# Moving the split weights of an encoder block by 64 bytes against their partner operand

## The chip, the cores and the metric

The kernel runs on one core of one Trainium2 chip. The metric is the device time of one execution in microseconds (us). Before the change it is 1420.87 us, the median of 3 runs (1420.75 to 1421.65).

## The reference

One layer of a streaming encoder over 512 tokens of width 2048, all in float32. Cut to what matters:

```python
h = rmsnorm(x, norm_w)                                   # (512, 2048)
a_q, a_f, a_i, a_g, c_q, c_kv, k_idx, w_idx, b_g, m_a, m_b = split(h @ w_in)   # w_in: 2048 x 10128
y_a = rmsnorm(hgrn2_recurrence(silu(a_q), 1 - f(a_f), log f(a_f), a_i)) * silu(a_g)  # 8 heads of 128
q, q_idx = (rmsnorm(c_q) @ w_uq), (rmsnorm(c_q) @ w_qidx)     # c_q has 512 columns
k, v = split(rmsnorm(c_kv) @ w_ukv)
y_b = attention(q, top_k(indexer(q_idx, k_idx, w_idx)) of (k, v), rel_bias) * silu(b_g)
merged = sigmoid(m_a) * (y_a @ w_pa) + sigmoid(m_b) * (y_b @ w_pb)
out = rmsnorm(x + merged @ w_out) * final_norm_w
```

Nearly all of the arithmetic is products of 512 tokens with weight matrices.

## The kernel before

**Split products.** TensorE multiplies float32 numbers in a fast format with a shorter mantissa (`float32r`, FR in the code). To keep float32 accuracy each operand is split into a high part and the rest: `split` (L66) writes the high part with ScalarE (ACT, L67) and the rest with VectorE (DVE, L68). A product is then three matmuls, written by `mm3` (L70): high by high (L71), one rest by high (L72), high by the other rest (L73). In each matmul one operand, 128 columns wide, is loaded into the array by a weight load (LDWEIGHTS, the engine row PEld): the **stationary** operand. The other streams through it, 256 or 512 columns here: the **moving** operand. In the profile a matmul is named out<-moving,stationary, or the other way round; which is which is in the code: the first operand of `PE.matmul(ps, l, r)` is the stationary one. Each matmul has its own weight load, which runs while the matmul ahead of it streams.

**Where the work lies.** Weights come in pieces of at most 128 x 1024 float32 by DMA (SyncE's queue, SP) into tiles `wr` of the pool `weights`, and are split into the tiles `wh` and `wl` of that pool. `specs` lists the pieces in the order of use. `prep(i)` (L149) splits pieces up to two ahead of the one in use; the pool has three buffers of `wh` and `wl`. TensorE's order is the program's order. Small work of other stages (attention, the recurrence, top-k) is pumped in between by `pump`.

The program's stages that matter here:

- **Gate units** (`pair_job`, `pair_unit`, L929 and after): 11 units of 8 steps; each step has 42 matmuls of 256 columns (7 products of Strassen's scheme, 2 column halves, 3 matmuls). Seven products need three plain blocks of the weights (split into `bh`, `bl`) and four sums of blocks (`pair_sums`: VectorE L138 to L140 adds, then `wh`, `wl`). Weights are stationary, the tokens (`xh`, `xl`, and their sums `sh`, `sl`) move. At the end of a unit `gate_pair_evac` (L970) takes the seven sums out of PSUM: VectorE L975 to L981. For the first four units, whose gate is a silu, VectorE also multiplies four times (L987) by a sigmoid of ScalarE, in the unit after. Seven of the eight PSUM banks are in use, so a unit's fifth product needs a bank that L979 of the evacuation sets free.
- **a_i jobs** (`ai_job`): 3 jobs of 192 matmuls of 256 columns. The tokens are stationary, the weights `wh`, `wl` move.
- **Out units** (`out_job`, `pair_unit` with `tokens_out`): 3 units of 8 steps of 42 matmuls of 256 columns for 1536 of the 2048 output columns. The merged tokens (`mh`, `ml`, and their sums `so`) are stationary, the weights (`bh`, `bl`, `wh`, `wl`) move.
- **Other products** have 512 columns (`feat_job`: weights stationary, tokens move) or 384 (the indexer's). Of those, `uqkv` multiplies the normalised c_q (`cqh`, `cql`) by w_uq: 96 matmuls of 512 columns in 4 jobs.

Of the kernel before, what the change touches and what calls it, by code (L numbers as in the profile page):

```python
# [26 lines left out]
F32 = mybir.dt.float32  # L27
FR = mybir.dt.float32r
# [6 lines left out]
T, D = 512, 2048  # L35
# [3 lines left out]
NEG = -1e30  # L39
GONE = -3e38  # L40
WCAP = 1024
MO = (0, 128, 384, 768)


@with_exitstack
def hybrid_block(ctx, tc, x, norm_w, w_in, lb_table, gnorm_a, q_norm_w, kv_norm_w, w_uq,
# [3 lines left out]
    V, A, G, PE, SP = nc.vector, nc.scalar, nc.gpsimd, nc.tensor, nc.sync  # L50
# [25 lines left out]
        PE.matmul(ps, l, r, start=first, stop=last, skip_group_check=True)  # L76


    ident = const.tile([128, 128], F32, name="ident")
    levels = const.tile([128, 6, 32], U8, name="levels")  # L80
    A.dma_start(ident, c_ident)
    ones = const.tile([128, 128], F32, name="ones")
    G.memset(ones, 1.0)
    ones_r = const.tile([128, 128], FR, name="ones_r")
    G.tensor_copy(ones_r, ones)
    eps = const.tile([128, 1], F32, name="eps")
    G.memset(eps, EPS)
    cols = const.tile([128, 32], F32, name="cols")
# [16 lines left out]
    def enter(name, side=None, space=None):  # L105
        cm = tc.tile_pool(name=name, bufs=1, side=side, reuse_waits="tile")
        pools[name] = (cm, cm.__enter__())
        return pools[name][1]
# [4 lines left out]
    R = SimpleNamespace()  # L113
# [14 lines left out]
    def load_ahead():  # L128
        while issued[0] < min(issued[1] + 2, len(specs)):
            load(issued[0])  # L130
            issued[0] += 1

    def pair_sums(t):


        b = t.rearrange("p (q n) -> p q n", q=4)
        sv = R.g.tile([128, 4, 256], F32, name="sv", bufs=R.sv)
        V.tensor_tensor(sv[:, 0:2, :], b[:, 1:3, :], b[:, 0:1, :].to_broadcast([128, 2, 256]), op=OP.add)  # L138
        V.tensor_tensor(sv[:, 2, :], sv[:, 1, :], b[:, 1, :], op=OP.add)  # L139
        V.tensor_tensor(sv[:, 3, :], sv[:, 2, :], b[:, 3, :], op=OP.add)  # L140
        bh = R.g.tile([128, 3, 256], FR, name="bh", bufs=3)
        bl = R.g.tile([128, 3, 256], FR, name="bl", bufs=3)
        split(bh, bl, b[:, 1:4, :])
        vh = wpool.tile([128, 4, 256], FR, name="wh")
        vl = wpool.tile([128, 4, 256], FR, name="wl")
        split(vh, vl, sv)
        return bh, bl, vh, vl

    def prep(i):  # L149
        while issued[1] < min(i + 3, len(specs)):  # L150
            j = issued[1]
            if specs[j][3:] == ("pair",) and not hasattr(R, "g"):
                open_pairs()
            load_ahead()
            _, kc, n = specs[j][:3]
            t = raws.pop(j)
            if specs[j][3:] == ("pair",):
                halves[j] = pair_sums(t)
                issued[1] += 1
                continue  # L160
            if len(specs[j]) > 3:
                both = R.s2.tile([128, 2, WCAP], FR, name="wk", tag=specs[j][3])
                hi, lo = both[:, 0, :], both[:, 1, :]
            else:
                hi = wpool.tile([128, WCAP], FR, name="wh")
                lo = wpool.tile([128, WCAP], FR, name="wl")
            split(hi[:, :kc * n], lo[:, :kc * n], t[:, :kc * n])
            halves[j] = tuple(a[:, :kc * n].rearrange("p (k n) -> p k n", k=kc) for a in (hi, lo))
            issued[1] += 1
# [26 lines left out]

    jobs, hg = [], {}

    def feat_job(src, col, ntile, nk, kc, rhs, evac, before=None, width=T, after=None):
        at = len(specs)  # L200
        n = ntile * 128
        for k in range(0, nk, kc):
            specs.append(([(0, n, src[k * 128:(k + kc) * 128, col:col + n])], kc, n))

        def run():
            if before:
                before()
            ps = [mmp.tile([128, T], F32, name="acc")[:, 0:width] for _ in range(ntile)]
            for i in range(nk // kc):
                prep(at + i)  # L210
                wh, wl = halves.pop(at + i)
                for c in range(ntile):
                    for k in range(kc):
                        kk = i * kc + k
                        rh, rl = rhs(kk)
                        s = slice(c * 128, c * 128 + 128)
                        mm3(ps[c], wh[:, k, s], wl[:, k, s], rh, rl, kk == 0, kk == nk - 1)
                    if kk == nk - 1:
                        evac(c, ps[c])
                    if ntile < 4 or c % 2:  # L220
                        pump()
                if after and i in after:
                    after[i]()

        jobs.append(run)
# [8 lines left out]
    def start():  # L234
        R.v0 = enter("v0")
        p0 = enter("p0", side="right")
        HF = D // 2
        nw = p0.tile([16, 128], F32, name="nw")
        wc = p0.tile([128, 16], F32, name="wc")
# [3 lines left out]
        sq = p0.tile([128, HF], mybir.dt.bfloat16, name="sq")  # L243
        st = p0.tile([128, 4, 4], F32, name="st")
        rows = p0.tile([128, 128], F32, name="rows")
        wh = [p0.tile([128, 4, 272], FR, name=f"fh{i}") for i in range(4)]
        wl = [p0.tile([128, 4, 272], FR, name=f"fl{i}") for i in range(4)]
        raw = [None] * 4
# [167 lines left out]
    def open_branches():  # L416
        R.v = enter("values")
        R.s = enter("shared")
        R.q = enter("idx", side="right")
        R.M = R.s.tile([128, 1280], F32, name="M")  # L420
        R.ckh = R.s.tile([128, 2, T], FR, name="ckh")
        R.ckl = R.s.tile([128, 2, T], FR, name="ckl")
        lev = R.q.tile([128, 6, 32], F32, name="lev", tag="bf")
        SP.dma_start(lev, c_levels.rearrange("p (l t) -> p l t", l=6))
        G.tensor_copy(levels, lev)
# [159 lines left out]
    def ai_job(p):  # L585
        at = len(specs)
        c0 = 2048 + p * 256
        for k in range(0, NK, 4):
            specs.append(([(0, 256, w_in[k * 128:(k + 4) * 128, c0:c0 + 256])], 4, 256))

        def run():
            ps = [mmp.tile([128, T], F32, name="acc") for _ in range(2)]
            for i in range(4):
                prep(at + i)
                wh, wl = halves.pop(at + i)
                for k in range(4):
                    kk = i * 4 + k
                    rh, rl = x_rhs(kk)
                    for t in range(4):
                        s = slice(t * 128, t * 128 + 128)  # L600
                        mm3(ps[t // 2][:, (t % 2) * 256:(t % 2) * 256 + 256], rh[:, s], rl[:, s],
                            wh[:, k, :], wl[:, k, :], kk == 0 and t % 2 == 0, kk == NK - 1)
                    if k % 2 == 1:
                        pump()
            v = hg[p, "v"] = R.v.tile([128, 4, 256], F32, name="hv", bufs=2)
            for i in range(2):
                A.activation(v[:, 2 * i:2 * i + 2, :], ps[i].rearrange("p (t n) -> p t n", t=2), AF.Copy)

        jobs.append(run)
# [24 lines left out]
    def hgrn_gen(p):  # L634
# [54 lines left out]
        for c in range(2):  # L689
            pt = bank("hkt")  # L690
            for j in range(3):
                PE.transpose(pt[:, j * 128:(j + 1) * 128], k[:, c, j * 128:(j + 1) * 128], ident)
            A.activation(kd[:, c], pt[:, :384].rearrange("p (j t) -> p j t", j=3), AF.Copy)
        yield
        st = R.h.tile([128, 2, 3, 128], F32, name="hst")
# [138 lines left out]
    def att_turn(blocks):  # L834
        bk = [bank("tA"), bank("tB"), bank("tC")]
        hi = R.a.tile([128, 1280], FR, name="PT")
        for kt in range(4):
            for b in range(kt, 4):
                o = PT_AT[kt] + (b - kt) * 128
                PE.transpose(bk[o // 512][:, o % 512:o % 512 + 128],  # L840
                             blocks[b][:, kt * 128:kt * 128 + 128], ident)
        lo = R.a.tile([128, 1280], FR, name="P")
        for i, o in enumerate((0, 512, 1024)):
            s = slice(o, min(o + 512, 1280))
            split(hi[:, s], lo[:, s], bk[i][:, 0:s.stop - o])
        return hi, lo
# [56 lines left out]
    def open_pairs():  # L903
        drain("norm")
        drain("misc")
        leave("norms")
        R.g = enter("pairs")
        R.sv = 2

    xs_h, xs_l = [], []  # L910

# [145 lines left out]
        feat_job(w_in, p * 256, 2, NK, 4, x_rhs, aq_evac(p))  # L1057

    def uqkv(p):
        feat_job(w_uq, p * 256, 2, 4, 4, c_rhs, uq_evac(p),  # L1060
                 before=None if p else (lambda: drain("top")))
        ukv_job(p)

# [59 lines left out]
    def open_merge():  # L1123
        drain("att")
        flush()
        flush()
        leave("att")
        leave("shared")
        leave("values")
        leave("us")  # L1130
        leave("ranks")
        R.m = enter("merged")
        R.s2 = enter("sums2")
        R.u = enter("us")
        R.g = enter("pairs", side="right")
        R.sv = 1
        load_gates(32, 0)
        load_gates(16, 0)

# [258 lines left out]
```

## Time and profile before

| | |
|---|---|
| median of 3 runs | 1420.87 us (1420.75 to 1421.65) |
| the profiled execution's own time | 1417.68 us |
| its span in the profile | 1415.9 us |
| busy share of the span | PE 98%, PEld 90%, DVE 75%, ACT 43%, POOL 6% |
| chain that ended last | PE 79%, DVE 11%, ACT 5%, DMA 2% |

Between span and own time lie 1.8 us. The profiled execution is 3.2 us below the median of the runs. Matmuls are pipelined, and the durations of the profile overlap: how fast TensorE gets on is read from the starts of successive matmuls.

### The profile page before, as it was taken

To read this page: it belongs to the slowest core of one execution; us is meant where nothing else is said; L and a number is where in the kernel's file an instruction comes from. 1 tells how busy PE (TensorE), PEld (TensorE's weight loads), DVE (VectorE), ACT (ScalarE), POOL (GpSimd) and SP (SyncE) were. 2 spreads that over 40 slices of the span, in tenths; PEclk is the share of its full clock that TensorE was granted. 3 is DMA by queue.
4 is the path that set the end of the run, shared out by engine and by line. 5 is a ranking of instruction groups with operands and counts; after the bars stand their busy time and mean duration, and the time that the engine had idled before them with its cause. 6 is when DMAs were issued, how large, how long until landed. Compare 5 with 4: busy or idle time off the path is not lost.

```text
span 1415.9 us, 25873 instructions
## 1 busy us (share of the span) xinstructions
PE 1392.4 (98%) x10652; PEld 1276.0 (90%) x10652; DVE 1059.4 (75%) x1736; ACT 606.9 (43%) x857; POOL 88.3 (6%) x85
## 2 busy tenths in 40 slices
PE   8999999999999999999999999999999999999997
PEld 7878999999999999997888889988888888899996
DVE  7877888889888887677769966577655438899856
ACT  6455444444444344564142352454353224443334
POOL 2100000000000000000201211213111000000000
PEclk9999999999999999999999999999999999999999
DMA  6223344444443444324324243334466556743554
GB/s 214 82 83 118 106 135 134 128 127 150 135 133 104 137 135 133 123 82 135 106 68 137 78 131 106 97 119 128 164 227 230 175 194 220 227 134 116 169 183 173
DMA packets 138776, 197.30 MB, mean 139 GB/s; under 512 B 9841, under 2 KB 82082, under 8 KB 138530
## 3 DMA queue, kind: packets, MB, share of 16 engines
q1 hardware_dynamic: 137266, 194.27, 44.0%
q8 instruction: 83, 1.36, 0.4%
q10 hardware_dynamic: 1392, 1.39, 0.3%
q14 instruction: 35, 0.29, 0.1%
HBM read 163.63 MB, written 31.99 MB: 138 GB/s over the span
## 4 chain that ended last, share of the span: by engine, by line
PE 79%; DVE 11%; ACT 5%; DMA 2%; issue 2%; POOL 0%; SPq 0%; ACTq 0%; DVEq 0%; POOLq 0%
PE acc L71 13%; PE acc L73 13%; PE acc L72 13%; PE pp L71 10%; PE pp L73 10%; PE pp L72 10%; ACT wh L67 3%; DVE wl L68 2%; PE hl L76 1%; PE acc L76 1%; DVE sv L138 1%; DMA wr<-in_w_pa_dram 1%; PE ho L76 1%; DVE sv L139 1%; DVE sv L140 1%
## 5 line engine op out<-in xcount | busy, mean ns | idle before, releaser
L67 ACT ACTIVATE wh<-wr 128x1024 fp32r<-128x1024 f32 (+1 forms) x120 | 125.0, 1043 | 219.6 <-PE acc L72 69.1
L68 DVE TENSOR_TENSOR wl<-wr,wh 128x1024 fp32r<-128x1024 f32 (+1 forms) x120 | 146.3, 1220 | 94.5 <-ACT wh L67 92.9
L67 ACT ACTIVATE wh<-sv 128x1024 fp32r<-128x1024 f32 x112 | 118.5, 1058 | 177.5 <-DVE sv L140 167.4
L71 PE MATMUL acc<-xh,wh 128*128 128x512 f32 x432 | 173.1, 401 | 0.0
L73 PE MATMUL acc<-xh,wl 128*128 128x512 f32 x432 | 168.6, 390 | 0.0
L72 PE MATMUL acc<-xl,wh 128*128 128x512 f32 x432 | 168.2, 389 | 0.0
L68 DVE TENSOR_TENSOR wl<-sv,wh 128x1024 fp32r<-128x1024 f32 x112 | 137.3, 1226 | 27.8 <-ACT wh L67 27.8
L71 PE MATMUL pp<-sh,wh 128*128 128x256 f32 x528 | 149.6, 283 | 0.7 <-DVE c L979 0.7
L67 ACT ACTIVATE bh<-wr 128x768 fp32r<-128x768 f32 x112 | 94.0, 839 | 130.2 <-issue 62.5
L72 PE MATMUL pp<-sl,wh 128*128 128x256 f32 x528 | 149.4, 283 | 0.0
L73 PE MATMUL pp<-sh,wl 128*128 128x256 f32 x528 | 149.4, 283 | 0.0
L68 DVE TENSOR_TENSOR bl<-wr,bh 128x768 fp32r<-128x768 f32 x112 | 106.8, 954 | 30.7 <-ACT bh L67 30.1
L71 PEld LDWEIGHTS pp<-sh,wh 128*128 128x128 f32 x528 | 101.3, 192 | 1.2 <-issue 1.2
L72 PEld LDWEIGHTS pp<-sl,wh 128*128 128x128 f32 x528 | 101.3, 192 | 0.0
L73 PEld LDWEIGHTS pp<-sh,wl 128*128 128x128 f32 x528 | 101.3, 192 | 0.0
L71 PE MATMUL acc<-yh,wh 128*128 128x512 f32 x256 | 99.9, 390 | 0.0
L73 PE MATMUL acc<-yh,wl 128*128 128x512 f32 x256 | 99.7, 389 | 0.0
L73 PE MATMUL pp<-xh,bl 128*128 128x256 f32 x352 | 99.6, 283 | 0.0
L72 PE MATMUL pp<-xl,bh 128*128 128x256 f32 x352 | 99.6, 283 | 0.0
L72 PE MATMUL acc<-yl,wh 128*128 128x512 f32 x256 | 99.6, 389 | 0.0
L71 PE MATMUL pp<-xh,bh 128*128 128x256 f32 x352 | 99.6, 283 | 0.0
L71 PEld LDWEIGHTS acc<-xh,wh 128*128 128x128 f32 x432 | 81.1, 188 | 18.0 <-issue 2.1
(379 smaller groups left out, 3649.8 us busy)
## 6 DMA issues: line engine op xcount, KB each, us to landing
wr<-in_w_in_dram SPq DMA_DIRECT2D x152, 512.0 KB, 3.7
wr<-in_w_out_dram SPq DMA_DIRECT2D x32, 512.0 KB, 4.1
mg<-gate_d SPq DMA_DIRECT2D x48, 256.0 KB, 4.1
gate_d<-c SPq DMA_DIRECT2D x44, 256.0 KB, 4.2
wr<-in_w_pa_dram SPq DMA_DIRECT2D x16, 512.0 KB, 4.9
wr<-in_w_pb_dram SPq DMA_DIRECT2D x16, 512.0 KB
x<-in_x_dram SPq DMA_DIRECT2D x8, 512.0 KB, 6.3
wr<-in_w_qidx_dram SPq DMA_DIRECT2D x8, 512.0 KB, 5.1
```

The source lines that it names most:

```text
L67: A.activation(hi, src, AF.Copy)
L68: V.tensor_tensor(lo, src, hi.bitcast(F32), op=OP.subtract)
L71: PE.matmul(ps, lh, rh, start=first, stop=False, skip_group_check=True)
L72: PE.matmul(ps, lh, rl, start=False, stop=False, skip_group_check=True)
L73: PE.matmul(ps, ll, rh, start=False, stop=last, skip_group_check=True)
L76: PE.matmul(ps, l, r, start=first, stop=last, skip_group_check=True)
L138: V.tensor_tensor(sv[:, 0:2, :], b[:, 1:3, :], b[:, 0:1, :].to_broadcast([128, 2, 256]), op=OP.add)
L139: V.tensor_tensor(sv[:, 2, :], sv[:, 1, :], b[:, 1, :], op=OP.add)
L140: V.tensor_tensor(sv[:, 3, :], sv[:, 2, :], b[:, 3, :], op=OP.add)
```

## The change

**What it does to places.** A tile's start byte within a partition decides where an operand begins. In the built program before, all these tiles start at 32 mod 128, except the two c_q tiles, and `bh`, `bl` of the out units, which start at 96. A matmul's slices start at multiples of 512 bytes within a tile, so a tile's residue is that of its operands. The change widens every `wh` and `wl` tile by 64 float32 numbers and takes 1024 of them from a chosen place: 0, 16 (`STILL`, 64 bytes) or 48 (`MOVED` and `RANK`, 192 bytes). A tile `gap` of 16 numbers shifts `bh` and `bl` of the gate units by 64 bytes. The distance of the moving operand from the stationary one, mod 128 bytes, changes so:

| products | matmuls | columns | stationary starts at | moving starts at | distance |
|---|---|---|---|---|---|
| gate units | 3696 | 256 | 32, now 96 | 32 | 0, now 64 |
| a_i jobs | 576 | 256 | 32 | 32, now 96 | 0, now 64 |
| out units, weights `wh`, `wl` | 576 | 256 | 32 | 32, now 96 | 0, now 64 |
| out units, weights `bh`, `bl` | 432 | 256 | 32 | 96 | 64, as before |
| w_uq | 96 | 512 | 32, now 96 | 96 | 64, now 0 |
| other weights of 512 columns | some 2250 | 512 | 32 | 32 | 0, as before |

To make room, the tile `ident` (the identity for transposes) is no longer kept from start to end: one copy lies in the pool of the start, a second one is loaded for the later stages. `ones` is no longer a tile of its own but `ones_r` read as float32. Some 160 transposes of 128 columns get another distance by this (32 or 96, now 64).

```diff
+STILL, MOVED, RANK = 16, 48, 48
...
-    ident = const.tile([128, 128], F32, name="ident")
-    A.dma_start(ident, c_ident)
-    ones = const.tile([128, 128], F32, name="ones")
-    G.memset(ones, 1.0)
-    G.tensor_copy(ones_r, ones)
+    ones = ones_r.bitcast(F32)
...
+    def weight_places(at):
+        return [wpool.tile([128, WCAP + 64], FR, name=name)[:, at:at + WCAP] for name in ("wh", "wl")]
...
-        vh = wpool.tile([128, 4, 256], FR, name="wh")
-        vl = wpool.tile([128, 4, 256], FR, name="wl")
+        vh, vl = (a.rearrange("p (q n) -> p q n", q=4) for a in weight_places(R.at))
...
-                hi = wpool.tile([128, WCAP], FR, name="wh")
-                lo = wpool.tile([128, WCAP], FR, name="wl")
+                hi, lo = weight_places(*specs[j][3:] or (0,))
...
+        ident = p0.tile([128, 128], F32, name="ident")
+        A.dma_start(ident, c_ident)
...
+        G.memset(rows, 1.0)
+        G.tensor_copy(ones_r, rows)
...
+        R.ident = R.s.tile([128, 128], F32, name="ident")
+        SP.dma_start(R.ident, c_ident)
...
-            specs.append(([(0, 256, w_in[k * 128:(k + 4) * 128, c0:c0 + 256])], 4, 256))
+            specs.append(([(0, 256, w_in[k * 128:(k + 4) * 128, c0:c0 + 256])], 4, 256, MOVED))
...
-        R.sv = 2
+        R.g.tile([128, STILL], F32, name="gap")
+        R.sv, R.at = 2, STILL
...
-        feat_job(w_uq, p * 256, 2, 4, 4, c_rhs, uq_evac(p),
+        feat_job(w_uq, p * 256, 2, 4, 4, c_rhs, uq_evac(p), place=RANK,
...
-        R.sv = 1
+        R.sv, R.at = 1, MOVED
```

**What moves in order.** On TensorE, VectorE and ScalarE every instruction keeps its place. Two places differ on the other queues. GpSimd (POOL) at the start of the program, before:

```order
L1394 UNCONDITIONAL_BRANCH
L83 MEMSET ones 128x128
L85 CAST ones_r<-ones 128x128
L87 MEMSET eps 128x1
L273 MEMSET rows 128x128
```

and now:

```order
L1401 UNCONDITIONAL_BRANCH
L86 MEMSET eps 128x1
L248 MEMSET rows 128x128
L249 CAST ones_r<-rows 128x128
L277 MEMSET rows 128x128
```

The first four matmuls of the program (`warm`, L272), which read `ones`, now stand behind the cast instead of the first memset. SyncE's queue (SP) after the last gate unit, where `gate_d<-c` are the stores of its results and `wr` the loads of the next weights, before:

```order
L990 DMA gate_d<-c_6474 128x2x256
L990 DMA gate_d<-c_6473 128x2x256
L424 DMA lev<-in_levels_dram 128x192
L125 DMA wr<-in_w_qidx_dram 128x4x256 x5
L125 DMA wr<-in_w_in_dram 128x4x256 x3
```

and now:

```order
L997 DMA gate_d<-c_6474 128x2x256
L997 DMA gate_d<-c_6473 128x2x256
L428 DMA ident<-in_ident_dram 128x128
L430 DMA lev<-in_levels_dram 128x192
L124 DMA wr<-in_w_qidx_dram 128x4x256 x5
L124 DMA wr<-in_w_in_dram 128x4x256 x3
```

One load of 64 KB stands there in addition, ahead of the same loads.

## Rows read from the trace of the kernel before

**Rows 1.** The page, busy time by engine and granted clock in 40 slices.

```profile
PE 1392.4 (98%) x10652; PEld 1276.0 (90%) x10652; DVE 1059.4 (75%) x1736; ACT 606.9 (43%) x857; POOL 88.3 (6%) x85
...
PEclk9999999999999999999999999999999999999999
```

**Rows 2.** Waits of PE, longest total first: us, times, longest.

```profile
PE pt L293 <- DMA x<-in_x_dram: 2.4, 1, 2.4
```

**Rows 3.** PE's timeline at the start of the fifth gate unit: start, duration (us).

```profile
290.39 0.28 PE L71 MATMUL pp<-xh,bh 128*128 128x256 f32 x1
...
293.03 0.28 PE L72 MATMUL pp<-sl,wh 128*128 128x256 f32 x1
...
293.77 0.35 PE L71 MATMUL pp<-sh,wh 128*128 128x256 f32 x1 [0.34 <-DVE c L979]
```

**Rows 4.** PE's timeline of one step of the third out unit.

```profile
1328.64 0.28 PE L71 MATMUL pp<-bh,mh 128*128 128x256 f32 x1
...
1328.99 0.28 PE L71 MATMUL pp<-bh,mh 128*128 128x256 f32 x1
...
1330.01 0.28 PE L71 MATMUL pp<-wh,so 128*128 128x256 f32 x1
...
1332.15 0.29 PE L71 MATMUL pp<-bh,so 128*128 128x256 f32 x1
...
1333.56 0.28 PE L71 MATMUL pp<-bh,mh 128*128 128x256 f32 x1
```

**Rows 5.** PE's timeline in two stretches of 512 columns: w_uq, then w_pb.

```profile
794.04 0.39 PE L72 MATMUL acc<-cql,wh 128*128 128x512 f32 x1
...
795.67 0.39 PE L73 MATMUL acc<-cqh,wl 128*128 128x512 f32 x1
...
1150.02 0.39 PE L71 MATMUL acc<-yh,wh 128*128 128x512 f32 x1
...
1154.56 0.39 PE L73 MATMUL acc<-yh,wl 128*128 128x512 f32 x1
```

**Rows 6.** Groups of PE by form: count, busy us, mean ns of one.

```profile
L71 PE MATMUL pp<-sh,wh 128*128 128x256 f32 x528 | 149.6, 283 | 0.7 <-DVE c L979 0.7
...
L72 PE MATMUL pp<-bl,mh 128*128 128x256 f32 x96 | 26.7, 278 | 0.0
```

**Rows 7.** DVE's timeline from the first to the fifth evacuation of a gate unit.

```profile
166.53 0.69 DVE L975 TENSOR_TENSOR c<-pp,c 128x512 f32<-128x512 f32 x1
...
290.22 0.68 DVE L975 TENSOR_TENSOR c<-pp,c 128x512 f32<-128x512 f32 x1
...
292.94 0.68 DVE L979 TENSOR_TENSOR c<-pp,c 128x512 f32<-128x512 f32 x1
...
298.68 0.68 DVE L987 TENSOR_TENSOR c<-c,sg 128x512 f32<-128x512 f32 x1
...
303.45 0.69 DVE L138 TENSOR_TENSOR sv<-wr 128x512 f32<-128x512 f32 x1
...
306.25 1.23 DVE L68 TENSOR_TENSOR wl<-sv,wh 128x1024 fp32r<-128x1024 f32 x1 [0.32 <-ACT wh L67]
...
331.08 0.68 DVE L975 TENSOR_TENSOR c<-pp,c 128x512 f32<-128x512 f32 x1
```

**Rows 8.** PE's timeline: the first matmul of the second and of the sixth gate unit.

```profile
169.15 0.28 PE L71 MATMUL pp<-xh,bh 128*128 128x256 f32 x1
...
331.26 0.28 PE L71 MATMUL pp<-xh,bh 128*128 128x256 f32 x1
```

**Rows 9.** Windows: stretch and its us, then busy us (count) of PE, PEld, DVE, ACT, POOL; clock, DMA share, GB/s.

```profile
372.10:573.70 201.60, 201.60 (x1682) 201.60 (x1681) 161.75 (x228) 84.94 (x104) 0.00 (x0) 1.00 0.43 129
...
682.00:711.00 29.00, 29.00 (x608) 27.74 (x607) 26.15 (x44) 4.90 (x6) 9.55 (x6) 1.00 0.26 77
...
1242.50:1283.00 40.50, 39.90 (x338) 39.49 (x336) 36.84 (x54) 17.15 (x23) 0.00 (x0) 1.00 0.43 134
```

**Rows 10.** PE's timeline: the first matmul of the second out unit.

```profile
1282.95 0.39 PE L71 MATMUL pp<-bh,mh 128*128 128x256 f32 x1 [0.53 <-ACT hv L1221]
```

More of the change, by code (lines that the diff above doesn't have):

```diff
@@ L160, in prep @@
                 continue
-            if len(specs[j]) > 3:
+            if len(specs[j]) > 3 and isinstance(specs[j][3], str):
                 both = R.s2.tile([128, 2, WCAP], FR, name="wk", tag=specs[j][3])
@@ L197, in hybrid_block, with feat_job @@
     jobs, hg = [], {}
-    def feat_job(src, col, ntile, nk, kc, rhs, evac, before=None, width=T, after=None):
+    def feat_job(src, col, ntile, nk, kc, rhs, evac, before=None, width=T, after=None, place=0):
         at = len(specs)
@@ L202, in feat_job @@
         for k in range(0, nk, kc):
-            specs.append(([(0, n, src[k * 128:(k + kc) * 128, col:col + n])], kc, n))
+            specs.append(([(0, n, src[k * 128:(k + kc) * 128, col:col + n])], kc, n, place))
         def run():
@@ L691, in hgrn_gen @@
             for j in range(3):
-                PE.transpose(pt[:, j * 128:(j + 1) * 128], k[:, c, j * 128:(j + 1) * 128], ident)
+                PE.transpose(pt[:, j * 128:(j + 1) * 128], k[:, c, j * 128:(j + 1) * 128], R.ident)
             A.activation(kd[:, c], pt[:, :384].rearrange("p (j t) -> p j t", j=3), AF.Copy)
@@ L840, in att_turn @@
                 PE.transpose(bk[o // 512][:, o % 512:o % 512 + 128],
-                             blocks[b][:, kt * 128:kt * 128 + 128], ident)
+                             blocks[b][:, kt * 128:kt * 128 + 128], R.ident)
         lo = R.a.tile([128, 1280], FR, name="P")
```

## The prediction

> **What bounds the kernel now.** The page comes first: TensorE is busy 98% of the span, at the full granted clock (2.4 GHz, the upper level) in every slice, and VectorE 75% [rows 1]. The waits of PE come second: the longest is 2.4 us in the first 6 us, the others are smaller [rows 2]. So the time is nearly the number of matmuls times the interval between their starts, and a change that adds and removes no matmul can only alter that interval, or the few waits.
>
> The interval is not a busy time, because durations overlap; it is read from the timeline. In a gate unit 22 matmuls of 256 columns start between 290.39 and 293.03 [rows 3]: 2.64 / 22 = 120.0 ns each. 256 columns at 2.4 GHz would be 106.7 ns, so 13 ns of each are something else. The out units hold the natural experiment. They use the same shape on the same operand kinds, but there the weights `bh`, `bl` already lie 64 bytes away from the stationary tokens, while `wh`, `wl` lie on the same residue. The timeline of one step shows both within 5 us [rows 4]: from 1328.99 to 1330.01 nine matmuls with distance 64 take 1.02 us, 113.3 ns each; from 1330.01 to 1332.15 eighteen with distance 0 take 2.14 us, 118.9 ns each. The groups by form agree: 283 ns against 278 ns of mean duration [rows 6]. At 512 columns it is the other way: distance 0 (w_pb) makes 20 matmuls in 4.54 us, 227 ns each; distance 64 (w_uq) makes 7 in 1.63 us, 233 ns each [rows 5].
>
> The Trainium skill speaks against this change ("TensorE: Matmul & The Clock Gate", "Step-by-step: what each phase is for"): TensorE has two independent SBUF read ports, and loading the next weights takes no read bandwidth from the running matmul. By that rule a distance between the two operands would change nothing and the sum would be 1420.9 us. The trace does not agree: 113.3 against 118.9 and 120.0 ns within one kernel.
>
> **The change part by part.** Price per matmul: 120.0 - 113.3 = 6.7 ns, for products of 256 columns that go from distance 0 to 64. I take the steady value, since after the change whole units have one distance. The other end: in [rows 4] the first three matmuls at distance 64, just after others, took 0.35 us, 117 ns each. If the mean over a unit lay between, at 115.5 ns, the price would be 4.5 ns.
>
> *Gate units, 3696 matmuls.* On TensorE alone a unit of 336 goes from 40.32 to 38.08 us, 2.24 us less. That holds in unit 1 and in units 7 to 11, where VectorE has room: 161.75 us of 201.60 [rows 9], 80%, which becomes 85%. It does not hold in units 2 to 5. There VectorE also multiplies the silu gates, and sets the pace already. Its timeline shows one evacuation begin at 290.22 and the next at 331.08 [rows 7]: 40.86 us, more than TensorE's 40.32, with evacuation, silu (298.68 to 303.45) and eight preparations in between. From the first evacuation (166.53) to the fifth (331.08) it needs 164.55 us, which do not depend on TensorE's interval. What is left to gain is at the ends of this stretch.
>
> - Its start hangs on TensorE: the evacuation's first VectorE step needs the third product of unit 1's last step, 24 matmuls before the unit's end. It begins 169.15 - 166.53 = 2.62 us before unit 2 does [rows 7, 8]. At the new interval 24 x 6.7 ns less: 2.46 us.
> - Its end: the fifth evacuation begins 331.26 - 331.08 = 0.18 us before unit 6 does. Now TensorE is ahead, held twice per unit. In step 4 it waits for the rests `wl` that VectorE finishes at 306.25 + 1.23 = 307.48, 17.3 us after the evacuation began. The first matmul that reads them is the 15th of the step, so 196 follow or run: 196 x 113.3 ns = 22.2 us. The unit ends 39.5 us after its evacuation began, and the next evacuation begins at 40.86: 1.4 us after the unit's start instead of 0.18 before.
>
> So from the start of unit 2 to that of unit 6 the time is 164.55 - 2.46 - 1.4 = 160.7 us, after 331.26 - 169.15 = 162.1 now: 1.4 us gained, where TensorE alone would give 9.0. Unit 6 pays a wait at its fifth product: L979 ends 292.94 + 0.68 - 290.22 = 3.4 us after the evacuation begins, 4.8 us after the unit begins; TensorE is there after 24 x 113.3 ns = 2.7 us and waits 2.1. Today such a wait is 0.5 us (293.77 instead of 293.27 [rows 3]). So unit 6 gains 2.24 - 1.6 = 0.6. Sum of the gates: 2.24 + 1.4 + 0.6 + 5 x 2.24 = 15.5 us.
>
> *a_i jobs, 576 matmuls:* 576 x 6.7 ns = 3.8 us. VectorE is busy 26.15 us of 29 there [rows 9], with the recurrence and top-k, so this may shrink, at worst to nothing if it falls behind; at 27.7 us per window it would be 94% busy, and I take the whole.
>
> *Out units.* A step of 42 now takes 1333.56 - 1328.64 = 4.92 us [rows 4]; at 113.3 ns each it is 4.76, 1.3 us less per unit. In the first unit VectorE is busy 36.84 of 40.50 us [rows 9], besides waits for ScalarE's half of each split. At its end TensorE waits for ScalarE's copy out of PSUM [rows 10], which stands in ScalarE's queue behind those splits: VectorE's and ScalarE's work sets the end of that unit, and its 1.3 us come back as a longer wait. Units 2 and 3: 2.5 us.
>
> *w_uq:* 96 matmuls of 512 columns go from 64 to 0: 96 x (233 - 227) = 0.6 us less.
>
> *The rest.* The cast ahead of the `warm` matmuls delays them by less than 1 us; behind it PE waits 2.4 us for the first input [rows 2], which covers it, and without that cover it would cost the delay. The second load of `ident` stands on SP ahead of loads that are needed a stage later; it waits for the last read of a tile of token sums, and the `lev` load behind it waits for the gate units' end anyway. The 160 transposes get a distance for which the rows have no pair; at 6.7 ns either way it is 1.1 us at most, and I take nothing.
>
> Sum: 15.5 + 3.8 + 2.5 + 0.6 = 22.4 us. The profiled execution's own 1417.7 us becomes 1395.3; it lies 3.2 us below the median of the runs, so the median goes from 1420.9 to 1398.5 us. With a price of 4.5 ns the gates give 1.5 + 1.8 + 7.6, the a_i jobs 2.6, the out units 1.5: 15.6 us with w_uq, 1405. If VectorE's stretch gives 2 us more, 1396. The likeliest case's own range is 1395 to 1405.
>
> **The rivals.**
>
> *VectorE does not hold the gates back* (0.08). Some of its 164.55 us may be waits for buffers that TensorE frees earlier now. For it: its total is only 3.3 us over TensorE's own 4 x 40.32 = 161.3. Against it: in the period 290.22 to 331.08 the idle pieces before its instructions name ScalarE, not PE [rows 7]. Units 2 to 6 would then gain up to 11.2 instead of 2.0 us, 1389.
>
> *The order of the two operands matters* (0.08). All matmuls at distance 64 and 256 columns here have the moving operand at 96 and the stationary one at 32. The gates get the reverse. For it: no row shows that order. Against it: 64 up and 64 down are the same mod 128. Then the gates stay at 120 ns and 6.9 us are left: 1414.
>
> *The change does nothing* (0.05): the 113.3 ns belong to the tiles `mh` and `bh`, not to the distance. Against it: the twelve matmuls from 1332.15 to 1333.56 [rows 4], six of `bh` with `so` (64) and six of `wh` with `mh` (0), take 117.5 ns each, between the two: it goes with the pair, not with either tile. 1421. The Trainium skill's rule of the two independent ports, named above, would give this time.
>
> *Slower* (0.05): the reversed order costs what distance 64 costs at 512 columns, 6.3 ns. All of it lies on the path: 3696 x 6.3 ns = 23.3 us more, 6.9 less elsewhere: 1437. It decides from an interval of 121.9 ns in the gates on (6.9 us / 3696 over 120.0).
>
> **How the numbers follow.** 0.74 is left for the forecast, 1398.5 us. With the first rival 0.82 lie between 1388 and 1406, which I take as the range. Under 0.2% (2.8 us) a measurement of this kernel cannot be told from no change. Faster: 0.74 + 0.08 + 0.08 = 0.90; same 0.05; slower 0.05.
>
> **What would show it.** In the gates' timeline starts 113 ns apart; units 7 to 11 at 38.1 us; units 3 to 5 still 40.9 us apart with PE waiting about 2.8 us in each, on L979 and on `wl`; in the first out unit a longer wait for L1221 or L1219; w_uq at 227 ns. Wrong would be starts 120 ns apart in the gates, or units 2 to 6 at 38 us.

## The result, and the profile after

The changed kernel takes 1410.1 us (median of four executions, 1409.04 to 1411.52) against 1420.8 us in the comparison on the same chip: ratio of the times, after to before, 0.9927, with a 95% interval from 0.991 to 0.9945. It is faster, by 10.7 us where 22.4 were forecast, and 1410.1 lies outside the forecast range of 1388 to 1406. The profiled execution took 1409.21 us (span 1407.4), 8.5 us less than that of before. The page and some of the longest waits of PE answer to [rows 1, 2]. Line numbers are those of each run's own kernel: L74 to L76 are the three matmuls of `mm3`, L986 is the evacuation's L979 of before, L1228 the copy L1221.

```profile
PE 1372.3 (98%) x10652; PEld 1253.6 (89%) x10652; DVE 1058.2 (75%) x1736; ACT 607.4 (43%) x857; POOL 89.1 (6%) x85
...
PEclk9999999999999999999999999999999999999999
```

```profile
PE pp L74 <- DVE c L986: 4.0, 4, 1.1
PE ho L79 <- DVE hst L709: 2.0, 1, 2.0
...
PE tA L846 <- DVE P L835: 1.7, 2, 1.3
PE pp L74 <- ACT hv L1228: 1.7, 1, 1.7
```

TensorE is busy 98% as before, but it waits longer than before: for the evacuation (L986, 4.0 us in sum instead of 0.7), for `hst`, a state of the recurrence (L709, 2.0 instead of 0.9), for the normalised scores `P` of the attention (L835, 1.7 us where the first profile of before had no such wait), and for `hv` (L1228, 1.7 instead of 0.5). PE's timeline shows the interval between the starts of successive matmuls. The four lines are the first matmul of gate unit 7, of gate unit 11, of out unit 3 and of the second step of out unit 3:

```profile
368.08 0.28 PE L74 MATMUL pp<-xh,bh 128*128 128x256 f32 x1
...
520.40 0.28 PE L74 MATMUL pp<-xh,bh 128*128 128x256 f32 x1
...
1314.88 0.28 PE L74 MATMUL pp<-bh,mh 128*128 128x256 f32 x1
...
1319.83 0.28 PE L74 MATMUL pp<-bh,mh 128*128 128x256 f32 x1
```

Four gate units, 1344 matmuls, take 520.40 - 368.08 = 152.32 us: 113.3 ns each, as forecast. The 42 of the out step take 4.95 us: 117.9 ns each, where the forecast had 113.3 and the kernel before 117.1 [rows 4]. All of these matmuls are at distance 64, and the granted clock is 1.00 in both stretches. So this distance gives not one interval but two.

The stages, each from its first matmul to the first of the next, in the profiled executions (before, after, and the change as forecast):

| stage | before | after | change | forecast |
|---|---|---|---|---|
| gate unit 1 | 40.30 | 38.26 | -2.04 | -2.24 |
| gate units 2 to 5 | 162.11 | 161.62 | -0.49 | -1.4 |
| gate unit 6 | 40.87 | 39.64 | -1.24 | -0.6 |
| gate units 7 to 11 | 201.60 | 190.40 | -11.20 | -11.2 |
| three a_i jobs | 87.96 | 85.37 | -2.60 | -3.8 |
| four uqkv jobs (with w_uq) | 60.32 | 62.58 | +2.25 | -0.6 |
| pa/pb | 185.93 | 190.85 | +4.92 | 0 |
| out unit 1 | 40.45 | 41.85 | +1.40 | 0 |
| out units 2 and 3 | 80.12 | 80.52 | +0.39 | -2.5 |

The rest changed by 0.1 us in sum.

### The profile page after: what moved, and what is told of

Same layout as the page of the kernel before. It is cut to its first block, busy times and chain, and to the rows that moved or that the text cites. A ratio compares the mean times of both kernels' runs of the same rounds, so it can differ in the third digit from the quotient of the medians.

```text
span 1407.4 us, 25875 instructions
## 1 busy us (share of the span) xinstructions
PE 1372.3 (98%) x10652; PEld 1253.6 (89%) x10652; DVE 1058.2 (75%) x1736; ACT 607.4 (43%) x857; POOL 89.1 (6%) x85
## 4 chain that ended last, share of the span: by engine, by line
PE 78%; DVE 11%; DMA 4%; ACT 4%; issue 3%; SPq 0%; POOL 0%; ACTq 0%; DVEq 0%; POOLq 0%
PE acc L74 12%; PE acc L76 11%; PE acc L75 11%; PE pp L74 11%; PE pp L76 11%; PE pp L75 11%; ACT wh L70 2%; DVE wl L71 2%; DMA wr<-in_w_pb_dram 1%; PE hl L79 1%; DMA wr<-in_w_pa_dram 1%; PE acc L79 1%; PE ho L79 1%; DVE mg L1186 1%; DMA mg<-gate_d 1%
## 5 line engine op out<-in xcount | busy, mean ns | idle before, releaser
L74 PE MATMUL acc<-xh,wh 128*128 128x512 f32 x432 | 173.1, 401 | 0.0
L76 PE MATMUL acc<-xh,wl 128*128 128x512 f32 x432 | 168.6, 390 | 0.0
L74 PE MATMUL pp<-sh,wh 128*128 128x256 f32 x528 | 146.6, 278 | 4.0 <-DVE c L986 4.0
L76 PE MATMUL pp<-sh,wl 128*128 128x256 f32 x528 | 146.6, 278 | 0.0
L75 PE MATMUL pp<-sl,wh 128*128 128x256 f32 x528 | 146.2, 277 | 0.0
L74 PEld LDWEIGHTS pp<-sh,wh 128*128 128x128 f32 x528 | 99.1, 188 | 4.7 <-issue 4.7
L76 PE MATMUL acc<-yh,wl 128*128 128x512 f32 x256 | 99.8, 390 | 0.4 <-DVE wl L71 0.4
L74 PE MATMUL acc<-yh,wh 128*128 128x512 f32 x256 | 99.9, 390 | 0.0
L76 PEld LDWEIGHTS pp<-sh,wl 128*128 128x128 f32 x528 | 99.5, 188 | 0.3
L74 PE MATMUL pp<-xh,bh 128*128 128x256 f32 x352 | 97.7, 277 | 1.1 <-ACT c L981 1.1
L76 PE MATMUL pp<-xh,bl 128*128 128x256 f32 x352 | 97.7, 278 | 0.4 <-DVE bl L71 0.4
L74 PEld LDWEIGHTS acc<-xh,wh 128*128 128x128 f32 x432 | 81.1, 188 | 18.0 <-issue 2.1
```

The lines of the kernel that those rows point to most:

```text
L74: PE.matmul(ps, lh, rh, start=first, stop=False, skip_group_check=True)
L75: PE.matmul(ps, lh, rl, start=False, stop=False, skip_group_check=True)
L76: PE.matmul(ps, ll, rh, start=False, stop=last, skip_group_check=True)
```

## The experiments

**Other executions of the same two kernels.** Kernel before, unchanged:

> The kernel before once more, for a second profile. Theory (the length of the pa/pb stage varies from one execution to the next, whatever the kernel): every other stage within 0.1 us of the first profile, pa/pb anywhere from 186 to 191 us instead of 185.93. Rival (it belongs to the edits): 185.9 us again.

Every stage up to pa/pb, the products with w_pa and w_pb, is within 0.12 us of the first profile (the start within 0.3), but pa/pb took 188.47 us instead of 185.93 and out unit 1 41.81 instead of 40.45; 1421.2 us. In pa/pb TensorE waits 1.2 us for `P` there too, which it did not in the first profile. Over the profiles of this study pa/pb takes 185.9 to 189.6 us without any change of distance and 185.9 to 190.9 us with one. Most of the 4.92 us is therefore variation between executions; what sets it was not found.

Changed kernel, unchanged:

> The changed kernel once more, for a second profile. Theory (at distance 64 a stream falls after a wait into one of two intervals, 113.3 or 117.8 ns, by chance, and keeps it until the next wait): gate units 7 to 11 all at 38.08 or all at 39.57 us, out units 2 and 3 all at 38.1 or all at 39.6, not tied to what the first profile had; pa/pb anywhere from 186 to 191. Rival (the interval is fixed by the program): 38.08 in gates 7 to 11 and 39.57 in out unit 3 again.

The theory held: the two places changed roles. PE's timeline, at the same four matmuls as above:

```profile
370.29 0.28 PE L74 MATMUL pp<-xh,bh 128*128 128x256 f32 x1
...
528.58 0.28 PE L74 MATMUL pp<-xh,bh 128*128 128x256 f32 x1
...
1320.67 0.28 PE L74 MATMUL pp<-bh,mh 128*128 128x256 f32 x1
...
1325.43 0.28 PE L74 MATMUL pp<-bh,mh 128*128 128x256 f32 x1
```

Now the gate units run at 158.29 us / 1344 = 117.8 ns and the out step at 4.76 us / 42 = 113.3 ns. The same program, the same addresses: which of the two a stream gets is settled in each execution. What settles it is open. Units 7 to 11 are worth 7.5 us by it (39.57 against 38.08 us each), out units 2 and 3 3.0 us. In this execution the gates gain 6.1 us in all and not 15, and out units 2 and 3 gain 2.5 us, the forecast. It took 1413.5 us.

**Which shift gives what.** Four kernels take shifts back. The first pair of lines is the out units' (in e_none, e_gates and e_noout), the second the a_i jobs' (e_none, e_gates, e_noai), the third that of w_uq (e_none, e_gates), the rest the gates' (e_none alone):

```diff
-        R.sv, R.at = 1, MOVED
+        R.sv, R.at = 1, 0
...
-            specs.append(([(0, 256, w_in[k * 128:(k + 4) * 128, c0:c0 + 256])], 4, 256, MOVED))
+            specs.append(([(0, 256, w_in[k * 128:(k + 4) * 128, c0:c0 + 256])], 4, 256, 0))
...
-        feat_job(w_uq, p * 256, 2, 4, 4, c_rhs, uq_evac(p), place=RANK,
+        feat_job(w_uq, p * 256, 2, 4, 4, c_rhs, uq_evac(p), place=0,
...
-        R.g.tile([128, STILL], F32, name="gap")
-        R.sv, R.at = 2, STILL
+        R.sv, R.at = 2, 0
```

> All four distances back to those of the kernel before; what is left of the change is the wider wh and wl tiles, the ident and ones tiles made elsewhere, and the second load of ident. Theory 1 (the longer pa/pb stage, 185.93 to 190.85 us, belongs to the distances or to work that runs earlier because of them): pa/pb 186 us, every stage as before, ratio 1.000 and 1421 us. Theory 2 (pa/pb is longer because of the moved tiles and the second load): pa/pb 190 to 191 us, ratio 1.0035 and 1426 us. Theory 3 (it varies from one execution to the next): ratio 1.000 with a pa/pb of either length in the profile.

Ratio 1.0004 (0.9995 to 1.0013), every stage within 0.1 us of before except start and tail (up to 0.2) and pa/pb (189.60). What the change does beside the distances costs nothing.

> Only the gate units keep their new distance of 64 bytes; a_i jobs, w_uq and out units are back as before. If the stages add up: gates 15 us shorter, a_i jobs 2.6 longer than in the changed kernel, first uqkv job 17.1 us again and no drop of the clock in it, out units as before; with pa/pb at 186 us 1406 us, ratio 0.9895; with pa/pb at 191 us 1411 us, ratio 0.993. Rival: the steps of the gate units at 117 to 118 ns depend on what stands elsewhere, and the gates differ from 448 us by over 2 us.

1416.3 us, ratio 0.9964 (0.995 to 0.9977), a miss: units 7 to 11 took 39.57 us each, the long interval. Six executions reach from 1412.4 to 1418.6. The first uqkv job was 17.14 us again.

> Everything as changed, only the out units' wh and wl back at distance 0. Theory (at distance 64 the stream there holds 117.7 ns and not 113.3, and the pair sums alternate anyway): steps of 4.92 us again, out units 1.8 us shorter than in the changed kernel, 1408.3 us, ratio 0.9912 if the rest stays. Rival (the 64 bytes help, and the out units were held by VectorE alone): out units no shorter than in the changed kernel, 1410 to 1412 us.

1411.9 us, ratio 0.9932 (0.992 to 0.9944). The out steps are those of before, as expected; gate units 7 to 11 took 39.57 us, which was not.

> Everything as changed, only the a_i jobs back at distance 0. Theory (VectorE's chain, top-k behind the recurrence, sets the start of the first uqkv job's ho products, so that the a_i jobs' gain comes back there): a_i jobs 2.6 us longer than in the changed kernel, wait of ho for hst 0.9 instead of 2.0 us and no clock drop behind it, first uqkv job 17.1 us: total within 0.5 us of the changed kernel, 1410 us, ratio 0.9925. Rival (the two have nothing to do with one another): first uqkv job stays at 19.7 us and the total is 1412.7 us, ratio 0.9943.

1412.1 us, ratio 0.9943 (0.9927 to 0.9958), gate units 7 to 11 at 39.57 and out units 2 and 3 at 39.56 and 38.08 us. The theory on the uqkv job fell: with the a_i jobs at their old speed it still takes 18.06 us (`e_noout`: 18.16). It is not VectorE falling behind in the a_i jobs. Over all profiles the three a_i jobs take 85.0 to 85.5 us with the shift and 87.9 to 88.0 without it: this gain of 2.5 us came every time.

**What puts a stream at 113.3 ns.** In the profiles a stream of distance 64 takes one of the two intervals when it restarts after a wait. Some go over from 117.8 to 113.3 later without a wait that the trace shows (gate unit 4 of the changed kernel after 108 matmuls, at the start of its fourth step); none in the gate and out units was seen to go back for good without a wait, though one of 0.05 us was enough (gate unit 2 of e_again). In the kernel before, the fast nine of [rows 4] stand behind matmuls at distance 0. So the next kernel puts six matmuls of each unit at distance 0, in its first step, behind the waits.

```diff
-        vh, vl = (a.rearrange("p (q n) -> p q n", q=4) for a in weight_places(R.at))
-        split(vh, vl, sv)
+        kick = 0 if R.pairs % 8 else 16
+        R.pairs += 1
+        last = R.at + 768 + kick
+        whole = [wpool.tile([128, WCAP + 64], FR, name=name) for name in ("wh", "wl")]
+        for at, q, n in ((R.at, 0, 3), (last, 3, 1)) if kick else ((R.at, 0, 4),):
+            split(*(a[:, at:at + n * 256].rearrange("p (q n) -> p q n", n=256) for a in whole), sv[:, q:q + n, :])
+        vh, vl = ([a[:, at:at + 256] for at in (R.at, R.at + 256, R.at + 512, last)] for a in whole)
...
-        R.sv, R.at = 2, STILL
+        R.sv, R.at, R.pairs = 2, STILL, 0
...
```

> The changed kernel, but in the first step of each gate and out unit the last quarter of wh and wl lies 64 bytes further, so that its six matmuls are at distance 0 and what follows is at 64; the split of that step is in two pieces. Theory (matmuls of distance 0 put the stream at 113.3 ns, as the nine in rows 4 show, and it stays there until the next wait): gate units 7 to 11 at 38.1 us and out units 2 and 3 at 38.1 us in every execution, 2.6 us less than before in the out units, 1402 to 1406 us, ratio 0.987 to 0.989, and a narrower spread of times. Rival (what follows six matmuls of distance 0 is left to chance too): 117.8 ns in some of these units, 1408 to 1412 us.

1399.1 us, ratio 0.9847 (0.9832 to 0.9862), four executions between 1397.9 and 1400.3: 11 us less than the changed kernel, with six matmuls per unit put back to the slow distance and the first split of each unit cut in two. The same four places in PE's timeline:

```profile
366.68 0.28 PE L74 MATMUL pp<-xh,bh 128*128 128x256 f32 x1
...
519.14 0.28 PE L74 MATMUL pp<-xh,bh 128*128 128x256 f32 x1
...
1305.03 0.28 PE L74 MATMUL pp<-bh,mh 128*128 128x256 f32 x1
...
1309.81 0.28 PE L74 MATMUL pp<-bh,mh 128*128 128x256 f32 x1
```

Both are at the short interval now: 152.46 us for four gate units, 4.78 us for the out step that has the six. The profiles of all six kernels with this edit show 38.11 us in each of units 7 to 11 and 38.12 in out unit 3; of the seven profiles without it that have the gates at 64 bytes, two have the short interval in units 7 to 11. Units 3 to 6 give more cases. Where such a unit waited for the evacuation in its first step, the steps 2 and 3 behind it ran at the short interval in 24 of 24 cases with the six matmuls and in 8 of 23 without. Only until the next wait, though: behind a wait in its fourth step gate unit 3 of e_kick ran at 117.8 ns. A control keeps the two-piece split and leaves the last quarter where it was:

```diff
-        last = R.at + 768 + kick
+        last = R.at + 768
```

> As e_kick, the split of the first step in two pieces, but the last quarter stays where the change has it, so that no matmul of these units is at distance 0. Theory (the six matmuls at distance 0 set the interval): states by chance again, gate units 7 to 11 and out units 2 and 3 at 38.1 or 39.6 us, several us between executions, 1403 to 1412 us and slower than e_kick by 4 us or more. Rival (the shorter wait of the two-piece split is what helped): 1399 us with 38.1 us in all these units.

Its six executions are 1397.8, 1398.3, 1403.7, 1409.7, 1411.4 and 1413.1 us: median 1406.7, ratio 0.991 (0.9879 to 0.994). The profiled one happens to have the short interval in gate units 7 to 11 and in the out units, and reaches e_kick's time. Without the distance-0 matmuls 15 us lie between executions of this kernel, with them 2.4, and the two intervals of the ratio do not meet. It is the distance of the six and not the pieces. (A narrow spread alone proves nothing: the changed kernel's four executions lie within 2.5 us, e_noout's five within 2.4, with long intervals in the profiles of both.)

**Other distances.**

```diff
-        R.g.tile([128, STILL], F32, name="gap")
-        R.sv, R.at = 2, STILL
+        R.g.tile([128, 8], F32, name="gap")
+        R.sv, R.at = 2, 24
```

> The changed kernel with the gate units' bh and bl 32 and wh and wl 96 bytes from the stationary residue instead of 64. Theory (only the residue mod 64 or mod 128 counts, 0 being the bad one): 113.3 or 117.8 ns as at 64 bytes, gate units 7 to 11 at 38.1 or 39.6 us. Rival (64 bytes is the one good distance): an interval near 120.0 ns in one or both, 40.3 us per unit where both.

Between the interval at distance 0 and the short one: 1413.6 us in its one execution, gate unit 1 takes 39.94 us (118.9 ns each), units 7 to 11 39.57 us (117.8 ns). No step of the gates at 32 and 96 bytes ran at 113.3 ns in this one profile. Whether they can is open.

**What holds gate units 2 to 6.** First without VectorE's silu multiplication (the first 16 gate blocks then hold the sigmoid alone):

```diff
-                    if j < 16:
+                    if j < 0:
```

> The changed kernel without VectorE's multiplication of the first 16 gate blocks by their sigmoid (units 1 to 4 put out the sigmoid alone). Theory (VectorE's chain of 40.86 us per unit sets the pace of units 2 to 6): TensorE no longer waits for L986 and wl there, each of these units takes 38.1 or 39.6 us by its interval, 201.3 us become 190.5 to 198. Rival (what holds the units is the restart after the evacuation, not VectorE's load): units 3 to 5 stay at 40.6 us or above.

All eleven units take 39.57 us, in a profile that got the long interval from the first unit on (1406.3 us); the waits for the evacuation are gone. The other four executions took 1388.6 to 1392.9 us; ratio 0.9788 (0.9769 to 0.9807). So the chain with VectorE's multiplication sets the pace there. Next the multiplication on GpSimd:

```diff
-                        V.tensor_tensor(c, c, g, op=OP.mult)
+                        G.tensor_tensor(c, c, g, op=OP.mult)
```

> As e_kick, with the silu multiplication of gate units 1 to 4 on GpSimd instead of VectorE. Theory (VectorE's chain sets the pace of units 2 to 6): VectorE's period per unit falls by the four multiplications of 0.69 us and the waits for the sigmoid between them, under 38 us; units 2 to 6 at 38.1 us, 199.6 us become about 191, 1390 to 1392 us, ratio 0.979. Rival (VectorE's instructions wait for GpSimd, as the copy of L691 did for L671): VectorE's other instructions become longer beside L999 and units 2 to 6 stay above 40 us, 1399 us or more.

1403.6 us, ratio 0.9883 (0.987 to 0.9895): the rival. Units 3 to 5 take 41.12 us. DVE's timeline, and POOL's beside it:

```profile
297.24 1.78 DVE L140 TENSOR_TENSOR sv<-wr 128x512 f32<-128x512 f32 x1
...
299.51 1.40 DVE L142 TENSOR_TENSOR sv<-sv,wr 128x256 f32<-128x256 f32 x1
```

```profile
296.66 1.81 POOL L999 TENSOR_TENSOR c<-c,sg 128x512 f32<-128x512 f32 x1 [33.08 <-ACT sg L998]
299.21 1.41 POOL L999 TENSOR_TENSOR c<-c,sg 128x512 f32<-128x512 f32 x1 [0.74 <-ACT sg L998]
```

L140 takes 1.78 us beside GpSimd's multiplication, 0.69 us elsewhere; L142 1.40 instead of 0.42. The Trainium skill ("SBUF — State Buffer", "Who interferes with whom") says that a VectorE instruction with two SBUF inputs and a GpSimd instruction that reads SBUF exclude each other; these rows agree. (Out unit 1 was 44.73 us here, with a 3.7 us wait for `mg`; it varies from 39.7 to 44.7 over all profiles.)

In e_kick itself DVE's timeline shows idle time between the multiplications:

```profile
295.56 0.68 DVE L999 TENSOR_TENSOR c<-c,sg 128x512 f32<-128x512 f32 x1
296.95 0.69 DVE L999 TENSOR_TENSOR c<-c,sg 128x512 f32<-128x512 f32 x1 [0.70 <-ACT sg L998]
298.34 0.69 DVE L999 TENSOR_TENSOR c<-c,sg 128x512 f32<-128x512 f32 x1 [0.70 <-ACT sg L998]
299.73 0.69 DVE L999 TENSOR_TENSOR c<-c,sg 128x512 f32<-128x512 f32 x1 [0.70 <-ACT sg L998]
```

ScalarE cannot start the next sigmoid before the multiplication has freed the only `sg`. A second `sg` takes the room of the second `sv`, whose last reader is done before VectorE writes the next (in the lines below it ends at 289.95 + 1.23 = 291.18, the next write begins at 293.69):

```diff
-            g = R.g.tile([128, 2, 256], F32, name="sg")
+            g = R.g.tile([128, 2, 256], F32, name="sg", bufs=2)
...
-        R.sv, R.at, R.pairs = 2, STILL, 0
+        R.sv, R.at, R.pairs = 1, STILL, 0
```

> As e_kick, with two buffers for the sigmoid tile sg and one instead of two for sv. Theory (in units 1 to 4 VectorE idles three times 0.70 us between its silu multiplications, since the next sigmoid must wait for the multiplication to free the only buffer): these 2.1 us per unit go, VectorE's period falls from 40.5 to about 38.4 us, units 2 to 6 from 199.6 to 191 to 194 us, total 1391 to 1394 us, ratio 0.979 to 0.981. Rival (VectorE's own work fills the period): 199 us stay, 1399 us.

1392.3 us, ratio 0.9799 (0.9782 to 0.9816); of the kernels that leave nothing out none has a lower median. Units 2 to 6 take 193.9 us instead of 199.6, and the four multiplications run without a gap:

```profile
289.95 1.23 DVE L71 TENSOR_TENSOR wl<-sv,wh 128x1024 fp32r<-128x1024 f32 x1 [0.34 <-ACT wh L70]
291.09 2.68 DVE L999 TENSOR_TENSOR c<-c,sg 128x512 f32<-128x512 f32 x4
293.69 0.68 DVE L140 TENSOR_TENSOR sv<-wr 128x512 f32<-128x512 f32 x1
```

**The first uqkv job.** Its `ho` products wait for `hst`, which stands on VectorE behind four copies of L691. Their durations in ns (shortest, median, longest) in the changed kernel:

```profile
L691 DVE COPY hS<-hnear x4: 282/283/1051, 776.0 to 776.9; 32x256 f32<-32x256 f32 x4
```

and in e_gates, where the job is as short as before:

```profile
L691 DVE COPY hS<-hnear x4: 282/284/290, 786.6 to 787.5; 32x256 f32<-32x256 f32 x4
```

One copy of four takes 1.05 us. GpSimd's multiplication L671 runs then, from 776.68 on in the changed kernel, and the last copy starts at 776.93. In e_gates both start at 787.45; in e_noai, where one copy took 1.19 us, L671 starts at 786.93 and the copy 8 ns later. Where the two start together, the one that is first makes the other wait:

```profile
787.45 1.20 POOL L671 TENSOR_TENSOR hk<-hk,tot 128x512 f32<-128x512 f32 x1 [2.32 <-PE hl L79]
```

```profile
786.93 1.05 POOL L671 TENSOR_TENSOR hk<-hk,tot 128x512 f32<-128x512 f32 x1 [2.31 <-PE hl L79]
```

The first is e_gates, where GpSimd takes 0.15 us more; the second is e_noai. With w_uq alone taken back:

```diff
-        feat_job(w_uq, p * 256, 2, 4, 4, c_rhs, uq_evac(p), place=RANK,
+        feat_job(w_uq, p * 256, 2, 4, 4, c_rhs, uq_evac(p), place=0,
```

> As e_kick, with w_uq back at distance 64. Theory (with w_uq moved, one copy of L691 starts at the same time as GpSimd's L671 and lasts 1.05 to 1.2 us instead of 0.29, and the ho products wait 2.1 instead of 1.1 us, with or without a clock drop behind): the copy lasts 0.29 us, first uqkv job 17.1 instead of 18.1 us, the other three 0.1 us longer each: 0.6 us less than e_kick in the profile, up to 2 us less where e_kick's executions have the drop, ratio 0.9835 to 0.9845. Rival (the collision has to do with the a_i jobs): 18 us or more stay, and w_uq loses its 0.5 us.

1400.1 us, ratio 0.986 (0.9847 to 0.9873), first uqkv job 18.14 us: a miss. In every profile with the a_i jobs or w_uq moved and the copies on VectorE one of these copies was late, in none of those with neither moved (before, b_again, e_none, e_gates): moving either was enough to tip the tie. Then the copies on ScalarE:

```diff
-                    V.tensor_copy(S[h:h + 32, :, h:h + 32], near[h:h + 32])
+                    A.activation(S[h:h + 32, :, h:h + 32], near[h:h + 32], AF.Copy)
```

> As e_kick, the four copies hS<-hnear of 32 rows on ScalarE instead of VectorE. Theory (the fourth copy starts together with GpSimd's L671 and waits for it): VectorE's chain to hst is shorter by at least 0.8 us, the ho products wait 1.1 us or less instead of 1.9, first uqkv job 17.1 us or less instead of 18.1, 1 us less than e_kick. Rival (VectorE is late from the a_i jobs' higher speed, by what stands ahead of these copies): job at 18 us still.

The job takes 16.34 us, the wait for `hst` 0.20 us; 1397.1 us, ratio 0.9833 (0.9814 to 0.9853). The collision was the cause.

> Both edits. If they add up: units 2 to 6 at 191 to 194 us and the first uqkv job at 17.1 us, 1390 to 1393 us, ratio 0.978 to 0.9805. Rival: the earlier end of the gates shifts the later collision, and the second edit gives nothing.

The stages add up (193.9 us, 16.34 us, span 1388.5), but the median of five is 1392.6 us, ratio 0.981 (0.9792 to 0.9829), no better than e_kick_sg. The second edit saves 3.3 us of that job between these two profiles, and no gain of the median is shown; pa/pb and out unit 1 vary by as much.

## Why the prediction was wrong, step by step

**The step that failed: "I take the steady value, since after the change whole units have one distance".** The price of 6.7 ns is that of a stream at 113.3 ns. At distance 64 there is a second steady interval, 117.8 ns, worth 2.2 ns in the gates and -0.7 ns in the out units (mixed step 117.1 before), and which of the two a stream gets differs between executions of the same program. [Rows 4] could not show it: every run of `bh` there came behind products at distance 0, the very thing that e_kick needed to get 113.3 every time. The pessimistic end, 115.5 ns, lay between the short interval and three matmuls of passage; the long interval is beyond it. With the short interval everywhere e_kick measures 1399.1 us, 0.6 us from the forecast, partly by luck: its split in two pieces also eases VectorE (units 2 to 6 take 199.6 us instead of 201.3), which makes up for about what the first uqkv job loses.

In the first profile this step explains only part of the gap. There 8.5 us came instead of 22.4. Of the 13.9 us that are missing, 2.9 are the long interval in out units 2 and 3, and 0.5 the gates; 4.9 are pa/pb, 2.9 the uqkv jobs, 1.4 out unit 1 and 1.2 the a_i jobs. In the second profile the gates alone are 9.4 us short, 7.5 of them by the long interval in units 7 to 11. Which streams had it in the other executions behind the median is not known, since only two were profiled.

**Gates, 15.5 us:** 15.0 in the first profile, 6.1 in the second. In the first the mechanism was right: in units 1 and 7 to 11 starts 113 ns apart, and in units 3 to 6 a wait for the evacuation (four, 4.0 us in sum). That VectorE needs 164.55 us was true for this change, but I counted the waits for `sg` as VectorE's need: four multiplications of 0.68 us fill 2.7 of the 4.77 us that [rows 7] show from 298.68 to 303.45.

**a_i jobs, 3.8 us:** 2.6 measured. Of their 552 intervals 387 were near 113 ns, 104 near 118 ns; the mean of the 530 that hold no other work fell from 119.7 to 114.6 ns, 5.2 ns and not 6.7. VectorE did not hold them back: the 22 that do hold other work take 4.8 us in sum, as before.

**Out units, 2.5 us:** right in the second profile (2.5), -0.4 in the first. That unit 1 gives nothing was right, and its wait for `hv` (L1228) grew to 1.7 us [rows 10].

**w_uq, 0.6 us:** 0.3 in the three later jobs. In the first, 2.5 us more. The prediction had the rest at nothing and looked for no tie between VectorE and GpSimd; about 1 us is that collision, and about 1.5 us a lower clock behind the wait. Windows of the changed kernel (stretch, its us, busy us of PE, PEld, DVE, ACT, POOL, clock) show it:

```profile
787.62:789.92 2.30, 0.27 (x3) 0.08 (x1) 2.27 (x5) 0.01 (x1) 0.00 (x0) 1.00 0.15 12
790.70:794.40 3.70, 3.70 (x22) 3.70 (x21) 3.19 (x5) 1.69 (x3) 1.67 (x3) 0.57 0.84 261
```

After 2.3 us with three matmuls the mean granted clock was 0.57, most of it the lower level (1.2 GHz): 22 matmuls in 3.7 us. After an equal wait in e_noout, whose program is the same up to there, it stayed at 1.00 (34 matmuls in 3.7 us):

```profile
796.80:799.00 2.20, 0.32 (x3) 0.13 (x2) 2.20 (x4) 0.06 (x1) 0.00 (x0) 1.00 0.12 17
799.90:803.60 3.70, 3.70 (x34) 3.70 (x33) 3.14 (x5) 2.29 (x5) 1.84 (x4) 1.00 0.80 246
```

So this, too, differs between executions. Eleven profiles have a wait of 1.9 to 2.0 us for `hst`; in five of them the clock fell behind it and the first uqkv job took about 19.7 us, in six it did not and the job took about 18.1 us. In the four with a wait of 0.9 us it stayed at 1.00.

**Profile and median.** The first profile of before has the shortest pa/pb but one of this study (185.93 us), that of after the longest (190.85). By profiles the change gives 8.5 us, by medians 10.7.

**Rivals.** The order of the operands does not matter: the gates reach 113.3 ns with the stationary operand moved. The changed kernel is faster, so the distances count, against the Trainium skill's rule of two independent read ports ("TensorE: Matmul & The Clock Gate", "Step-by-step: what each phase is for"): by it e_none and the changed kernel, which differ in the distances alone, would take the same time, and their ratios are 1.0004 and 0.9927.

## What to carry to other kernels

Before a steady interval is taken from a trace, look at what came ahead of the stream that shows it: the same addresses may have a second interval, and the profile of one execution shows only one of them. When a change of this kind measures less than it should, profile it twice: here the two profiles of the same kernel had the long interval in different places. The spread of the executions can tell too, 15 us in e_pieces and 2.4 us in e_kick, but a narrow one does not rule a second interval out. Look for the waits between short instructions before moving the instructions to another engine: taking out the 0.7 us waits for the one `sg` brought 1399.1 down to 1392.3 us, while the same multiplications on GpSimd, beside which VectorE's additions took about 1 us longer, gave 1403.6 us.

## What the runs showed of the hardware that was not expected

- At 256 columns with the split operands 64 bytes apart (mod 128), TensorE's stream in the gate units has two intervals, 113.3 and 117.8 ns, with the granted clock at 1.00 in both; at distance 0 all three profiles have 120.0 alone. Behind a wait it runs at one or the other, and six matmuls at distance 0 led to 113.3 until the next wait in every profile that had them.
- A 32x256 copy of 0.28 us on VectorE took 1.05 to 1.19 us beside a GpSimd multiplication; in e_noai the copy had started 8 ns after it, and in e_gates, where both started at 787.45, the multiplication took 0.15 us longer instead.
- A wait of 2.0 us on TensorE was followed by some 3.7 us mostly at the lower clock in five profiles, and by full clock behind as long a wait in six.
